# The combination of attention groups queued behind the first branch on three queues, inverse blocks loaded first, and the last two expert blocks multiplied together tile by tile

## The chip, the core and the metric

The kernel runs on one core of one Trainium2 chip. The metric is the device time of one execution in microseconds. TensorE (PE), VectorE (DVE), ScalarE (ACT), GpSimd (POOL) and SyncE (SP) each work through an instruction stream of their own in order, and wait for each other through semaphores. DMA transfers are issued by the streams of SP and ACT here (and by POOL for gathers); the profile shows an issuing stream as SPq or ACTq.

## What is computed

One layer of an encoder for 512 tokens of width 1024, in float32:

```python
xn = rmsnorm(h)
(dq, dk, dv, dz, da, db, aq, ak, av, gate_dn, gate_da) = split_columns(xn @ w_in, IN_WIDTHS)
o_dn = deltanet_branch(...)            # branch A: gated delta rule, two directions
o_da = dilated_attention_branch(...)   # branch B: three (window, dilation) groups of four heads
merged = sigmoid(gate_dn) * (o_dn @ w_branch_dn) + sigmoid(gate_da) * (o_da @ w_branch_da)
h = h + merged @ w_out
h = h + peer_ffn(rmsnorm(h), ...)      # 8 heads, top 16 of 16384 single-neuron experts
return rmsnorm(h, norm_final)
```

The attention branch ends with a combination: for each of its four heads the outputs of the three groups are weighted by a softmax over the groups and added.

```python
wts = jax.nn.softmax(jnp.stack(lses), axis=0)
o = jnp.einsum('gbhs,gbhsd->bhsd', wts, jnp.stack(outs))
```

## The kernel before

A float32 product is made of three matmuls (`mm3`): every operand is split into a high part, which ACT casts (`whi`, `xhi`, ..., line 117), and a low part, which DVE subtracts (`wlo`, ..., line 118); the products high-high, low-high and high-low are summed in PSUM. Weights come in halves of 128x1024 through SP (`raw`, line 147), three in flight.

The order of each engine's instructions is made by a tile scheduler from the code and a simulated timeline, not by the code's order alone. `keep_in_program_order` holds one instruction at its place, `issue_after` keeps what is issued in its scope behind a given instruction.

Around the change the stages on TensorE are, in order: the last projections with the attention of the last group; **branch A** (`branch_a`), whose input is transposed and split and then multiplied by `w_branch_dn`; the **gate blocks `gb`** (`gates(1, "gb")`), four blocks of two outputs of 128x512, each evicted by ACT as `f` (tanh, line 645); **branch da** (`branch` with `merge`), with the combination's result `obhi`, `oblo` as its input; and **w_out**.

- `branch` makes eight outputs of 12 matmuls of 128x512 (`mmb`, two PSUM banks). For branch A `keep` loads the gate into `pa` by ACT's queue (`pa<-th_d`, line 662, four buffers), multiplies on DVE (line 663), and stores by SP's queue (`pa_d<-pa`, line 664).
- The combination (lines 807 to 822) takes for each head h and group g the weights `cb<-c_d` (line 812, four buffers) and the group's output `og<-og_d` (line 814, six buffers) by SP's queue; DVE multiplies (line 815) and adds (line 819); the sum is split to `obhi` (ACT) and `oblo` (DVE). The first multiplication is held in program order.
- For branch da `fetch` loads `tb<-th_d` and `pa<-pa_d` by ACT's queue two outputs ahead (line 840); `merge` takes the product, adds `pa` and splits (`mhi`, `mlo`).
- w_out multiplies `mhi`, `mlo` in groups by token tile n into `mmo` (two banks, shared with `mmb`); `hs`, the input x as one load of 2 MB on ACT's queue (line 873), is added to the products.

Far ahead of this the delta rule inverts block triangular matrices. Per step, `m_d`, `i_d` and four diagonal blocks `e_d` are loaded by SP (lines 556 to 562).

At the program's end the expert outputs are summed over 64 blocks in six PSUM banks `acc[n][e]` (three token tiles, two halves), 36 matmuls of 128x512 a block (line 1201). In the last block these are sorted by tile, and behind each tile's 12 `final` adds `hs` (line 1162), takes the mean square (ACT), nine small operations for the inverse root (DVE, lines 181, 183, 108, 111 and 112), a scale by it and the norm's weights (line 1167) and the store.

## Time and profile before

| | |
|---|---|
| median of three runs | 1882.56 us (1878.89 to 1886.22) |
| the profiled execution | 1880.62 us, its span 1878.8 us |
| mean granted TensorE clock | 0.991 of full speed |
| TensorE busy | 1831.0 us (97%) |
| VectorE, ScalarE, GpSimd busy | 75%, 40%, 19% |

The span goes from the first to the last instruction of the profiled execution; the time holds 1.8 us more around it. Durations and starts below come from that one execution.

### The profile page before, as it was taken

Reading aid. Unit: us, or ns where it says so; the run is one execution under the profiler, and the core shown is the slowest. Engines: PE = TensorE matmul, PEld = TensorE weight load, DVE = VectorE, ACT = ScalarE, POOL = GpSimd, SP = SyncE. Lnnn points to the kernel's source line nnn. Section 1 sums busy time; section 2 is a strip of 40 time slices with the busy share of each in tenths; the row PEclk is TensorE's granted clock in tenths of the full one; section 3 lists DMA queues with packets and bytes.
Section 4 is the critical chain, followed back from the end, with each engine's and each line's share of the span. In section 5 each row is a group of like instructions: output and inputs, shape, how many; then the busy total and the mean of one; then the engine's idle time right before and its main releaser. Section 6 shows DMA issues by size and latency. Waiting matters only on the chain.

```text
span 1878.8 us, 28071 instructions
## 1 busy us (share of the span) xinstructions
PE 1831.0 (97%) x10438; PEld 1621.2 (86%) x10438; DVE 1400.7 (75%) x2979; ACT 751.5 (40%) x1168; POOL 364.1 (19%) x274
## 2 busy tenths in 40 slices
PE   8999999999699999999999999999999999999997
PEld 7897788888588888999999999999999998888886
DVE  6776544555535698999999857778778888787787
ACT  4543333343223423456666643333333332333332
POOL 0000000000000000001013223344444454233331
PEclk9999999999899999999999999999999999999999
DMA  6346423324865322557679899899999999999983
GB/s 204 101 133 180 135 85 94 102 86 144 281 210 163 130 90 85 166 160 283 238 282 377 317 384 327 293 350 332 338 345 321 352 321 368 378 351 345 337 306 125
DMA packets 188978, 451.84 MB, mean 240 GB/s; under 512 B 25053, under 2 KB 79901, under 8 KB 187306
## 3 DMA queue, kind: packets, MB, share of 16 engines
q1 hardware_dynamic: 135848, 266.75, 43.0%
q0 software_dynamic: 36864, 134.23, 19.5%
q10 hardware_dynamic: 16130, 49.07, 7.1%
q8 instruction: 82, 1.34, 0.3%
q14 instruction: 54, 0.44, 0.1%
HBM read 390.04 MB, written 59.96 MB: 240 GB/s over the span
## 4 chain that ended last, share of the span: by engine, by line
PE 62%; DMA 2%; DVE 1%; ACT 0%; issue 0%; SPq 0%; DVEq 0%; ACTq 0%
PE acc L1201 28%; PE psu L159 27%; PE psq L159 4%; PE psw L1123 2%; DMA wt<-w_d 1%; PE pssc L1007 1%; DMA raw<-peer_u 1%; DVE hs L1167 0%; DVE wlo L118 0%; ACT stage L1126 0%; SPq L147 0%; DVE hs L1162 0%; PE pst L1098 0%; DVE ge L1189 0%; ACT whi L117 0%
## 5 line engine op out<-in xcount | busy, mean ns | idle before, releaser
L118 DVE TENSOR_TENSOR wlo<-raw,whi 128x1024 fp32r<-128x1024 f32 x356 | 424.5, 1220 | 130.5 <-ACT whi L117 100.8
L117 ACT CAST whi<-raw 128x1024 fp32r<-128x1024 f32 x356 | 357.9, 1049 | 226.0 <-PE psu L159 76.4
L909 POOL DMA_INDIRECT grow<-peer_u_rows,gidx x128 | 175.5, 1371 | 834.8 <-DVE code L1046 497.7
L1201 PE MATMUL acc<-whi,hhi 128*128 128x512 f32 x768 | 237.1, 391 | 3.3 <-ACT hhi L117 3.3
L1201 PE MATMUL acc<-wlo,hhi 128*128 128x512 f32 x768 | 238.1, 390 | 0.0
L1201 PE MATMUL acc<-whi,hlo 128*128 128x512 f32 x768 | 237.2, 389 | 0.0
L909 POOL DMA_INDIRECT grow<-peer_v_rows,gidx x128 | 179.1, 1399 | 271.6 <-DVE gacc L928 242.9
L159 PE MATMUL psu<-x2hi,whi 128*128 128x384 f32 x1024 | 207.1, 341 | 0.0
L159 PE MATMUL psu<-x2lo,whi 128*128 128x384 f32 x1024 | 206.2, 340 | 0.0
L159 PE MATMUL psu<-x2hi,wlo 128*128 128x384 f32 x1024 | 205.5, 340 | 0.0
L117 ACT CAST hhi<-ge 128x768 fp32r<-128x768 f32 x64 | 53.6, 838 | 345.5 <-PE acc L1201 261.9
L159 PEld LDWEIGHTS psu<-x2hi,whi 128*128 128x128 f32 x1024 | 181.5, 188 | 2.8 <-ACT ge L964 0.6
L159 PEld LDWEIGHTS psu<-x2hi,wlo 128*128 128x128 f32 x1024 | 181.7, 188 | 0.0
L159 PEld LDWEIGHTS psu<-x2lo,whi 128*128 128x128 f32 x1024 | 181.4, 188 | 0.0
L1201 PEld LDWEIGHTS acc<-whi,hhi 128*128 128x128 f32 x768 | 144.3, 188 | 31.9 <-ACT hhi L117 3.6
L1201 PEld LDWEIGHTS acc<-wlo,hhi 128*128 128x128 f32 x768 | 144.7, 188 | 30.8
L1201 PEld LDWEIGHTS acc<-whi,hlo 128*128 128x128 f32 x768 | 144.2, 188 | 30.0
L928 DVE SCALAR_TENSOR_TENSOR gacc<-grow,gact,gacc 128x1024 f32<-128x1024 f32 x127 | 162.7, 1281 | 8.2 <-DMA grow<-peer_v_rows,gidx 6.7
L920 DVE SCALAR_TENSOR_TENSOR grow<-grow,x2g 128x1024 f32<-128x1024 f32 x128 | 152.2, 1220 | 13.5 <-DMA grow<-peer_u_rows,gidx 13.5
L159 PE MATMUL mmc<-xhi,whi 128*128 128x512 f32 (+1 forms) x528 | 135.6, 397 | 1.7 <-ACT xhi L117 1.2
L159 PE MATMUL mmc<-xhi,wlo 128*128 128x512 f32 (+1 forms) x528 | 133.6, 389 | 0.0
L159 PE MATMUL mmc<-xlo,whi 128*128 128x512 f32 (+1 forms) x528 | 131.9, 388 | 0.0
(355 smaller groups left out, 2427.5 us busy)
## 6 DMA issues: line engine op xcount, KB each, us to landing
raw<-peer_u SPq DMA_DIRECT2D x128, 512.0 KB
raw<-peer_v SPq DMA_DIRECT2D x128, 512.0 KB
raw<-w_in SPq DMA_DIRECT2D x68, 512.0 KB
w_d<-stage ACTq DMA_DIRECT2D x12, 2048.0 KB
wt<-w_d SPq DMA_DIRECT2D x32, 768.0 KB
ge_d<-ge SPq DMA_DIRECT2D x33, 384.0 KB
ge<-ge_d SPq DMA_DIRECT2D x33, 384.0 KB
raw<-peer_wq SPq DMA_DIRECT2D x16, 512.0 KB
```

Source lines behind the costliest of these rows:

```text
L117: S.copy(hi, src)
L118: sub = V.tensor_tensor(lo, src, hi.bitcast(F32), op=ALU.subtract)
L159: PE.matmul(ps, lhs(k)[x], rhs(k)[y], start=i == 0, stop=i == 3 * n - 1)
L909: G.indirect_dma_start(out=t_, out_offset=None, in_=rows, in_offset=bass.IndirectOffsetOnAxis(ap=gidx[:, slot:slot + 1], axis=0))
L920: tc.keep_in_program_order(V.scalar_tensor_tensor(t_, t_, 1.0, x2g, op0=ALU.mult, op1=ALU.mult, accum_out=gact[:, s:s + 1]))
L928: tc.keep_in_program_order(V.scalar_tensor_tensor(gacc, t_, gact[:, s:s + 1], gacc, op0=ALU.mult, op1=ALU.add))
L1007: PE.matmul(ps[:, n, :], qh[:, j, n * P:(n + 1) * P], sk[:, j, :], start=True, stop=True)
L1123: PE.matmul(ps[:, t, :], e1[:, pair, :, one], ge_[i][:, pair, :, one], start=i == 0, stop=i == 1)
L1201: PE.matmul(acc[n][e], x[:, j, n * P:(n + 1) * P], y[:, j, e * 512:(e + 1) * 512], start=b == order[0] and j == 0 and x is hhi and y is vh ...
```

## The change

1. *Inverse blocks:* the loads of the four diagonal blocks `e_d` are written ahead of those of `m_d` and `i_d`.
2. *Combination:* all of it is issued inside the scope of `issue_after` for three instructions of branch A: its last `pa<-th_d` load on ACT's queue, its last multiplication on DVE, its last `pa_d` store on SP's queue. The held multiplication is released.
3. *`hs`:* its load moves from the start of w_out into `fetch(KD - 1)`, behind the last `pa<-pa_d` load of the merge.
4. *Last two blocks:* the next to last block's 36 matmuls are kept back and sorted by tile together with the last block's 36; a tile ends after 24.

```diff
--- before.py
+++ after.py
@@ -553,13 +553,13 @@
                 xt = d2.tile([P, H, P], F32, name="xt", tag="xt")
                 yt = d2.tile([P, H, P], F32, name="yt", tag="yt")
                 mt = d2.tile([P, H, P], F32, name="mt", tag="mt")
-                nc.sync.dma_start(f4(mt), m_d[d, n])
-                it = d2.tile([P, H, P], F32, name="it", tag="it", bufs=1)
-                nc.sync.dma_start(f4(it), i_d[d, n])
                 dst, oth = (xt, yt) if d == 0 else (yt, xt)
                 G.memset(dst, 0.0)
                 for b in range(4):
                     nc.sync.dma_start(dst[diag[b], :, diag[b]], e_d[d, b, n].rearrange("h r c -> r h c"))
+                nc.sync.dma_start(f4(mt), m_d[d, n])
+                it = d2.tile([P, H, P], F32, name="it", tag="it", bufs=1)
+                nc.sync.dma_start(f4(it), i_d[d, n])
                 V.transpose(f4(oth), f4(dst))
                 zt = zts[:, d]
                 for wd in (32, 64):
@@ -654,14 +654,16 @@
                         lambda k: (hi[:, k, :], lo[:, k, :]), 4)
                     use(b * 4 + i, ps)
 
+        ends = [None] * 3
+
         def branch_a():
             d2ctx.close()
             with tc.tile_pool(name="oaT", bufs=1, side="right") as oap:
                 def keep(i, ps):
                     t_ = oap.tile([P, T], F32, name="pa", tag="pa", bufs=4)
-                    nc.scalar.dma_start(t_, th_d[0, i])
-                    V.scalar_tensor_tensor(t_, t_, 1.0, ps, op0=ALU.add, op1=ALU.mult)
-                    nc.sync.dma_start(pa_d[i], t_)
+                    ends[0] = nc.scalar.dma_start(t_, th_d[0, i])
+                    ends[1] = V.scalar_tensor_tensor(t_, t_, 1.0, ps, op0=ALU.add, op1=ALU.mult)
+                    ends[2] = nc.sync.dma_start(pa_d[i], t_)
 
                 oahi = oap.tile([P, H, T], F32R, name="oahi")
                 oalo = oap.tile([P, H, T], F32R, name="oalo")
@@ -805,6 +807,9 @@
         obhi = obp.tile([P, H, T], F32R, name="obhi")
         oblo = obp.tile([P, H, T], F32R, name="oblo")
         cmb = obctx.enter_context(tc.tile_pool(name="cmb", bufs=6, side="right"))
+        behind_a = ExitStack()
+        for last_a in ends:
+            behind_a.enter_context(tc.issue_after(last_a.ins))
         for h in range(H):
             for g in range(3):
                 c = g * 4 + h
@@ -812,14 +817,13 @@
                 nc.sync.dma_start(cb, c_d[c:c + 1].to_broadcast([P, T]))
                 og = cmb.tile([P, T], F32, name="og", tag="og")
                 nc.sync.dma_start(og, og_d[g * 4 + h])
-                mul = V.tensor_tensor(og, og, cb, op=ALU.mult)
-                if c == 0:
-                    tc.keep_in_program_order(mul)
+                V.tensor_tensor(og, og, cb, op=ALU.mult)
                 if g:
                     V.tensor_tensor(o_, o_, og, op=ALU.add)
                 else:
                     o_ = og
             split(obhi[:, h, :], oblo[:, h, :], o_)
+        behind_a.close()
 
         gates(1, "gb")
 
@@ -837,9 +841,12 @@
                 pair = []
                 for nm, src in (("tb", th_d[1, i]), ("pa", pa_d[i])):
                     t_ = m2.tile([P, T], F32, name=nm, tag=nm)
-                    nc.scalar.dma_start(t_, src)
+                    fetched = nc.scalar.dma_start(t_, src)
                     pair.append(t_)
                 ahead.append(pair)
+                if i == KD - 1:
+                    with tc.issue_after(fetched.ins):
+                        nc.scalar.dma_start(hs, a["x"].rearrange("(n p) d -> p n d", p=P))
 
             def merge(i, ps):
                 if i == 0:
@@ -869,8 +876,6 @@
             w = wblock(a["w_out"][e], (KD, 256))
             if e == 3:
                 wq0 = wblock(a["peer_wq"][0], (KD, 256))
-            if e == 0:
-                nc.scalar.dma_start(hs, a["x"].rearrange("(n p) d -> p n d", p=P))
             for n in range(NT):
                 tk = slice(n * P, (n + 1) * P)
                 ps = psa.tile([P, 256], F32, name="mmo", tag="mm", bufs=2)
@@ -1170,6 +1175,7 @@
             order = list(range(NF, NB)) + list(range(NF))
             new = dict(kept)
             new.update({b: layer1(b) for b in range(NF, NF + AHEAD)})
+            todo = []
             for b in order:
                 if NF <= b < NB - AHEAD:
                     new[b + AHEAD] = layer1(b + AHEAD)
@@ -1193,16 +1199,20 @@
                         pass
                     nc.sync.dma_start(gfin, a["norm_final"].to_broadcast([P, D]))
                     final(NT - 1, [gacc[:, e * 512:(e + 1) * 512] for e in range(2)])
-                todo = [(j, n, x, y, e) for j in range(2) for n in range(NT - 1)
-                        for x, y in ((hhi, vhi), (hhi, vlo), (hlo, vhi)) for e in range(2)]
+                todo += [(j, n, x, y, e) for j in range(2) for n in range(NT - 1)
+                         for x, y in ((hhi, vhi), (hhi, vlo), (hlo, vhi)) for e in range(2)]
+                if b == order[-2]:
+                    pace(2)
+                    continue
                 if b == order[-1]:
                     todo.sort(key=lambda q: (q[1], q[4]))
                 for i, (j, n, x, y, e) in enumerate(todo):
                     PE.matmul(acc[n][e], x[:, j, n * P:(n + 1) * P], y[:, j, e * 512:(e + 1) * 512],
                               start=b == order[0] and j == 0 and x is hhi and y is vhi,
-                              stop=b == order[-1] and j == 1 and x is hlo)
-                    if b == order[-1] and i % 12 == 11:
+                              stop=b == order[-1] and i % 12 == 11)
+                    if b == order[-1] and i % 24 == 23:
                         final(n, acc[n])
+                todo = []
                 pace(5 if b >= NF else 2)
     ctx.close()
```

What the change does to each engine's order: TensorE's is the same but for the last 72 matmuls, GpSimd's is the same. SP's differs in one place, the combination; its rows for the inverse blocks are the same. ACT's and DVE's differ around the combination, the merge and the end. At the end DVE's order is now: the last addition of `acc`, one small operation and the scale of the second tile, the nine small operations and the scale of the last tile; before, the scale of the first tile stood ahead of that addition, and the small operations of the second tile and its scale were mixed with those of the last.

SP, from the store of the combination's weights `ct` on, before:

```order
L804 DMA c_d<-ct 12x512
L814 DMA og<-og_d 128x512 x4
L812 DMA cb<-c_d 128x512 x4
L814 DMA og<-og_d 128x512
L664 DMA pa_d<-pa 128x512 x2
L814 DMA og<-og_d 128x512
L812 DMA cb<-c_d 128x512 x2
L664 DMA pa_d<-pa 128x512
L812 DMA cb<-c_d 128x512
```

and after the change:

```order
L806 DMA c_d<-ct 12x512
L666 DMA pa_d<-pa 128x512 x4
L147 DMA raw<-w_in 128x1024 x2
L666 DMA pa_d<-pa 128x512 x4
L817 DMA cb<-c_d 128x512
L819 DMA og<-og_d 128x512
L817 DMA cb<-c_d 128x512
L819 DMA og<-og_d 128x512
L817 DMA cb<-c_d 128x512
```

The stores `pa_d` of branch A were between the loads of the combination; now all eight are ahead of the first `cb`, with one weight block's two halves `raw` among them.

ACT from the load of `hs` on, before:

```order
L873 DMA hs<-x 128x4x1024
L117 CAST whi<-raw 128x1024 x2
L117 CAST obhi<-og 128x512
L662 DMA pa<-th_d 128x512 x3
L117 CAST obhi<-og 128x512
L662 DMA pa<-th_d 128x512
L117 CAST obhi<-og 128x512
L117 CAST whi<-raw 128x1024 x2
L117 CAST obhi<-og 128x512
L840 DMA pa<-pa_d 128x512 x3
L645 ACTIVATE f<-mmc 128x512
L117 CAST whi<-raw 128x1024 x2
```

and in the changed program, from the merge's first `pa` loads on, through the first gate outputs `f`:

```order
L844 DMA pa<-pa_d 128x512 x3
L645 ACTIVATE f<-mmc 128x512
L117 CAST whi<-raw 128x1024
L645 ACTIVATE f<-mmc 128x512
L117 CAST obhi<-og 128x512
L844 DMA tb<-th_d 128x512
L117 CAST obhi<-og 128x512
L645 ACTIVATE f<-mmc 128x512
L117 CAST whi<-raw 128x1024 x2
L844 DMA tb<-th_d 128x512
L645 ACTIVATE f<-mmc 128x512
L117 CAST whi<-raw 128x1024
```

Before, `hs` and four casts `obhi` (one for each head) stood around branch A's loads `pa<-th_d`, ahead of the first gate output `f`. Now the first two casts stand behind the second `f`, ahead of the third, and the other two further on.

ACT in the changed program at the last loads of the merge:

```order
L844 DMA pa<-pa_d 128x512
L849 DMA hs<-x 128x4x1024
L844 DMA tb<-th_d 128x512
L123 ACTIVATE mhi<-tb 128x512 x2
L117 CAST whi<-raw 128x1024 x2
```

`hs` stands between the last load `pa` and the last load `tb`.

DVE at the end of the merge and the start of w_out, before:

```order
L851 SCALAR_TENSOR_TENSOR tb<-tb,mmb 128x512 x2
L852 TENSOR_TENSOR tb<-tb,pa 128x512 x2
L124 SCALAR_TENSOR_TENSOR mlo<-tb,mhi 128x512 x2
L851 SCALAR_TENSOR_TENSOR tb<-tb,mmb 128x512
L118 TENSOR_TENSOR wlo<-raw,whi 128x1024
L852 TENSOR_TENSOR tb<-tb,pa 128x512
L118 TENSOR_TENSOR wlo<-raw,whi 128x1024
L124 SCALAR_TENSOR_TENSOR mlo<-tb,mhi 128x512
L879 TENSOR_TENSOR hs<-hs,mmo 128x256 x4
```

and after the change:

```order
L858 SCALAR_TENSOR_TENSOR tb<-tb,mmb 128x512 x2
L859 TENSOR_TENSOR tb<-tb,pa 128x512 x2
L124 SCALAR_TENSOR_TENSOR mlo<-tb,mhi 128x512 x2
L118 TENSOR_TENSOR wlo<-raw,whi 128x1024 x2
L858 SCALAR_TENSOR_TENSOR tb<-tb,mmb 128x512
L859 TENSOR_TENSOR tb<-tb,pa 128x512
L124 SCALAR_TENSOR_TENSOR mlo<-tb,mhi 128x512
L884 TENSOR_TENSOR hs<-hs,mmo 128x256 x4
```

The two halves `wlo` (of w_out's second block) stood between the operations of the last `tb`; now both are ahead of its first.

## Rows read from the trace of the kernel before

**Rows 1.** The page: the span, and part 1, engines' busy time.

```profile
span 1878.8 us, 28071 instructions
...
PE 1831.0 (97%) x10438; PEld 1621.2 (86%) x10438; DVE 1400.7 (75%) x2979; ACT 751.5 (40%) x1168; POOL 364.1 (19%) x274
```

**Rows 2.** Waits of TensorE: us in total, times, longest us.

```profile
PE mmb L159 <- DVE pa L663: 15.0, 2, 12.4
...
PE pz L576 <- DMA z<-z_d: 2.8, 1, 2.8
```

**Rows 3.** Timeline of TensorE: start us, us, operation, idle time before and what ended it.

```profile
491.08 1.10 PE L159 MATMUL mmb<-oahi,wlo 128*128 128x512 f32 x4
...
499.10 1.09 PE L159 MATMUL mmb<-oahi,whi 128*128 128x512 f32 x4
...
500.96 1.10 PE L159 MATMUL mmb<-oahi,wlo 128*128 128x512 f32 x4
...
514.45 2.08 PE L159 MATMUL mmb<-oahi,whi 128*128 128x512 f32 x4 [12.39 <-DVE pa L663]
...
521.94 2.01 PE L159 MATMUL mmc<-xhi,whi 128*128 128x512 f32 x8
...
532.86 0.39 PE L159 MATMUL mmc<-xhi,whi 128*128 128x512 f32 x1
```

**Rows 4.** Windows: us, each engine's busy time, granted clock, DMA share, GB/s.

```profile
495.00:500.00 5.00, 5.00 (x16) 3.96 (x17) 4.68 (x7) 0.62 (x1) 0.00 (x0) 0.71 1.03 416
...
585.00:590.00 5.00, 3.78 (x20) 2.96 (x19) 4.15 (x7) 2.26 (x4) 0.00 (x0) 1.00 0.36 133
```

**Rows 5.** Timeline of ScalarE and its queue, in two windows.

```profile
488.96 0.43 ACTq L873 DMA_DIRECT2D hs<-x  x1
...
506.48 2.97 ACTq L662 DMA_DIRECT2D pa<-th_d  x3
...
509.48 0.62 ACT L117 CAST obhi<-og 128x512 fp32r<-128x512 f32 x1 [11.01 <-DMA og<-og_d]
...
523.16 0.62 ACT L117 CAST obhi<-og 128x512 fp32r<-128x512 f32 x1
...
582.92 0.33 ACTq L840 DMA_DIRECT2D pa<-pa_d  x1
...
588.88 1.98 ACT L117 CAST whi<-raw 128x1024 fp32r<-128x1024 f32 x2
```

**Rows 6.** Waits of SyncE's queue: us in total, times, longest us.

```profile
SPq L814 <- DMA hs<-x: 5.3, 1, 5.3
```

**Rows 7.** Timeline of SyncE's queue.

```profile
485.53 1.75 SPq L812 DMA_DIRECT2D cb<-c_d  x4
...
503.45 0.32 SPq L814 DMA_DIRECT2D og<-og_d  x1
```

**Rows 8.** Timeline of VectorE, in two windows.

```profile
513.71 0.69 DVE L663 SCALAR_TENSOR_TENSOR pa<-pa,mmb 128x512 f32<-128x512 f32 x1 [1.55 <-DMA pa<-th_d]
...
589.62 0.68 DVE L851 SCALAR_TENSOR_TENSOR tb<-tb,mmb 128x512 f32<-128x512 f32 x1
...
591.95 1.22 DVE L118 TENSOR_TENSOR wlo<-raw,whi 128x1024 fp32r<-128x1024 f32 x1
```

**Rows 9.** Timeline of TensorE at the start of w_out.

```profile
591.85 0.28 PE L159 MATMUL mmo<-whi,mhi 128*128 128x256 f32 x1
```

**Rows 10.** Timeline of VectorE at the program's end.

```profile
1853.44 0.15 DVE L181 SCALAR_TENSOR_TENSOR tot<-ms 128x1 f32<-128x1 f32 x1
...
1855.36 1.42 DVE L1167 SCALAR_TENSOR_TENSOR hs<-hs,rs,x2g 128x512 f32<-128x512 f32 x2
...
1869.50 0.68 DVE L1162 TENSOR_TENSOR hs<-hs,acc 128x512 f32<-128x512 f32 x1
...
1874.22 1.42 DVE L1167 SCALAR_TENSOR_TENSOR hs<-hs,rs,x2g 128x512 f32<-128x512 f32 x2
```

**Rows 11.** Timeline of TensorE: the last matmul.

```profile
1867.99 0.39 PE L1201 MATMUL acc<-whi,hlo 128*128 128x512 f32 x1
```

## The prediction

> **What bounds the kernel now.** I read the page first: TensorE is busy 1831.0 of 1878.8 us [rows 1]. So an edit pays only where TensorE stands still, where its clock is low, or behind its last matmul; what other engines save elsewhere is hidden. The second view is TensorE's waits. One row stands out [rows 2]: two waits for the multiplication of branch A (`pa`, DVE), 15.0 us together, the longer 12.4. The third is TensorE's timeline there [rows 3]. A group of four branch matmuls takes 0.93 (500.96 less 499.10, two groups). [...]
>
> Why it stands is in the queues. ACT issues the 2 MB load `hs<-x` at 488.96 [rows 5], before branch A's last four loads of `th_d`. SP then waits 5.3 us for that load, ahead of an `og` load [rows 6], and goes on at 503.45 [rows 7]: 14.5 us from issue to landing. ACT issues the `th_d` loads at 506.48 [rows 5] and DVE, which has `og*cb` products among its `pa` operations, does the next `pa` at 513.71 [rows 8], where TensorE resumes (514.45). Thus the combination and `hs` stand in the way of branch A on all three queues.
>
> **The change part by part.**
>
> *Inverse blocks.* The order of issue on SP is the same in both programs, so the price is 0. The most an edit there could win is the one wait for `z_d`, 2.8 [rows 2]; losing needs a moved row, and there is none.
>
> *Combination and hs out of branch A.* Afterwards all eight `pa_d` stores precede the first `cb`, and the four loads follow the first four operations. What could still stop branch A: a store and then a load, both of the first buffer, between the first `pa` operation and the fifth. With two banks the fifth is due when the seventh output begins, five outputs of 12 matmuls (2.8 each) after the first output's end: 14.0, less two operations of 0.7, leaves 12.6 for the pair. The worst load took 7.2 (506.48 to 513.71), with combination loads beside it; so 5.4 are left for the store even then, and I take the pair as fitting. Lower end: one more stop like the shorter of the two, 15.0 less 12.4, 2.6. I take the full **-18.8**.
>
> *The combination, now late.* It no longer lies under branch A but under the `gb` gates, which don't need it until branch da. A `gb` block takes 10.92 (521.94 to 532.86 [rows 3]). With the loss gone `gb` starts at 503.2, and its blocks at 503.2, 514.1, 525.0 and 535.9; branch da is due at 546.8. The first `cb` is issued behind the last `pa` operation (0.7) and its store (0.3 of issue): about 504.4. ACT's new order is the risk: the casts `obhi` are interleaved with the casts of the next gate weights and with the `f` evictions that free TensorE's banks. Head 1's cast stands ahead of the second weight half of the third block, head 2's and 3's further on, so the third block (525.0) cannot go on without head 1. Before, from the first `cb` issue (485.53) to the cast of head 1 (509.48) passed 24.0, to that of head 3 (523.16) 37.6 [rows 5, 7]. [...] Head 3 at 542.0 is in time for 546.8. Below: 0, if DVE, free of its waits, is faster still. I take **+3.5**, between 0.3 and 7.5 and near their middle: the pace holds one removed wait, but DVE also does the gates' `wlo` subtractions there, and a stop of some length costs the clock besides. SP's `raw` loads now stand ahead of `cb`; they are due in any case.
>
> *hs as a neighbour of the merge.* `hs` is now issued between the last `pa` load and the last `tb` load of the merge. In the old times that is 583.3, just behind `pa` at 582.92 [rows 5]. Two things follow. First, DVE's order puts both `wlo` halves of the second output weight ahead of the last merge operation on `tb` (its last rows in the section on the change). That operation frees the bank into which the second tile's output group goes at 591.85 [rows 9], and ran at 589.62 [rows 8]. After, the two weight casts (588.88, 1.98 for both [rows 5]) end at 590.86, the second `wlo` (1.22 [rows 8]) at 592.2, and `tb` (0.7) at 592.9: a stop of **1.1** at least. Second, the last `tb` load lies behind 2.1 MB. At the 416 GB/s of 495 to 500 [rows 4] these take 5.0, from 583.3 to 588.3; if the weight loads take half of the rate, until 593.3. Then come `tb`'s own 0.26 MB (0.6) and the operation (0.7): 589.6 or 594.6, so the stop is 1.1 or 2.8. [...] I take **+2.5**, near the shared rate: the 14.5 were spent where the DMA engines' share was 1.03 (495 to 500), and from 585 to 590 it is 0.36 without `hs` [rows 4].
>
> [...]
>
> What `hs` and the combination leave behind: w_out's sum needs `hs` after its first group, later than `tb`, so no further wait.
>
> *Last two blocks together.* 72 matmuls instead of 36 are sorted by tile, so a tile ends every 24 matmuls, not 12; their count and duration stay. The last block's data is needed earlier: its first matmul comes 22 into the 72, so 50 x 0.23 (a quarter of 0.93) ahead of the end, at 1856.9; its last `hlo` subtraction is done when DVE goes on at 1853.44 [rows 10] or just behind, 3 us ahead, so that costs nothing. Before, TensorE ends at T = 1867.99 + 0.39 = 1868.4 [rows 11]; DVE adds the last tile at 1869.50, 1.1 late, busy until then with the scale of the first tile, and ends its last scale at 1874.22 + 1.42 = T + 7.3, with the second tile's scale in between [rows 10]. After, the add starts at T + 0.05 (0.6), then 0.2 of the second tile's chain, its scale (1.34), nine small operations of the last tile (1.92, 1853.44 to 1855.36 [rows 10]) and the last scale (1.42): T + 5.5. **-1.7.** Bounds: -2.4 if that second scale, too, is out of the way by T (its matmuls end 24 x 0.23 = 5.4 before); -0.4 if six small operations of the second tile (1.3) still come behind T.
>
> *Sum.* The profiled execution took 1880.6 us. 1880.6 - 18.8 + 3.5 + 2.5 - 1.7 = 1866.1. The median of the three runs is 1.9 above that execution: **1868**.
>
> **The rivals.**
>
> [...]
>
> [...]
>
> [...]
>
> C. *Slower.* With no branch work between them, the twelve `cb` loads go through four buffers in three rounds, and SP stands in each round for a transfer, as it did once, 5.3 [rows 6]. Such waits shift the heads and, through ACT's order, the gates behind them. If they take the place of the +3.5, three of 6.0 ((18.8 + 1.7 - 2.5) / 3) use up the gain; from 9.1 each it is slower by over 0.5%, and three of 10 give 1895. For it: SP has waited 5.3 for one transfer. Against it: that was for 2 MB, and these are 256 KB each.
>
> D. *Nothing gained in branch A*, because the store and load of the buffers are slow by themselves (the 7.2 of rows 5 and 8 is not due to `hs`): three stops of 2.6 remain of the 18.8 and it ends at 1876.
>
> **How the numbers follow.** About 0.5%, 9.4 us, is what a measurement of this kernel can tell from no change: the border is 1873. Chances: the forecast 0.66, A 0.13, B 0.10, both or D 0.08, C 0.03. The likeliest has 1868. Its best corner: 1880.6 - 18.8 + 0 + 1.1 - 2.4 = 1860.5, in the median's terms 1862.4; the runs before scatter by 3.7 either way, so 1859 is the lower end. Upwards the range takes in A and the middle of B, 1876, and leaves out C, A and B together, and half of B and D, 0.15 in all. Faster: the forecast and nearly all of A, 0.78; same: B, both, D and the rest of A, 0.19; slower: C, 0.03.
>
> **What would show it.** Right: TensorE's waits hold no `mmb` for `pa` of over 1 us, and the groups of branch A run at 0.93; `gb` begins about 503. A wait of TensorE at the third `gb` block for an `f` eviction or `whi`, 0 to 5.6, sizes the term of the combination; one of an `mmo` for `tb`, 1 to 4, that of `hs`; the span's end less the last matmul, 10.8 before (1878.8 - 1868.0), is to be 9.1. Wrong: waits of `pa` that remain (D), a `tb` that waits for its load over 5 us (B), SP rows on `cb` of over 5 us each (C), or a new wait in a stage that the change does not touch.

## The result

| | median, us | runs | ratio to before, 95% interval |
|---|---|---|---|
| before | 1882.11 | 4 (1878.89 to 1886.22) | |
| after | 1870.28 | 4 (1864.55 to 1871.48) | 0.9930 (0.9902 to 0.9958) |
| after, a second time on another occasion | 1869.79 | 6 (1865.40 to 1874.60), before then 1882.13 | 0.9929 (0.9912 to 0.9947) |

The changed kernel is 12 us, 0.7%, faster. 1868 was forecast, with 1859 to 1876 as the range.

The profiled execution of the changed kernel took 1864.55 us and is the quickest of its four; its profile is read with that in mind. The page, with its span and the busy times of part 1:

```profile
span 1862.8 us, 28073 instructions
...
PE 1827.6 (98%) x10438; PEld 1618.9 (87%) x10438; DVE 1401.4 (75%) x2979; ACT 751.0 (40%) x1168; POOL 358.0 (19%) x274
```

16.0 less than in [rows 1], of which TensorE was busy 3.4 less: the rest it no longer stands idle. Its waits (us in total, times, longest us) answer to [rows 2]:

```profile
PE mmc L159 <- ACT f L645: 3.4, 1, 3.4
...
PE mmb L159 <- DVE tb L858: 2.1, 1, 2.1
...
PE pz L576 <- DMA z<-z_d: 2.1, 1, 2.1
...
PE mmo L159 <- DVE tb L858: 1.8, 1, 1.8
```

The two waits of branch A for `pa` (15.0) are gone. In their place two new rows stand: 3.4 for `f` in the gate blocks, and 1.8 of w_out for `tb`. The wait for `z_d` (2.1) is 0.7 shorter than before, with SP's order there unchanged; such differences are told of below. TensorE's timeline through branch A and the gates (start, us, instruction, idle time ahead of it and what ended it):

```profile
490.45 1.10 PE L159 MATMUL mmb<-oahi,wlo 128*128 128x512 f32 x4
...
491.38 1.09 PE L159 MATMUL mmb<-oahi,whi 128*128 128x512 f32 x4
...
499.79 2.01 PE L159 MATMUL mmc<-xhi,whi 128*128 128x512 f32 x8
...
525.14 3.48 PE L159 MATMUL mmc<-xhi,whi 128*128 128x512 f32 x8 [3.39 <-ACT f L645]
...
528.46 2.00 PE L159 MATMUL mmc<-xlo,whi 128*128 128x512 f32 x8
```

The branch's groups now follow each other at 0.93 without a break (490.45 to 491.38), where [rows 3] had a stop of 12.4 and behind it four matmuls in 2.08, at a granted clock of 0.50 (514.5 to 518.3). The `gb` blocks begin at 499.79. The stop is in the third block, at 525.14: 3.39 of standing, and then eight matmuls in 3.48 where the next eight take 2.00, at a granted clock of 0.50 (525.2 to 528.0) and 1.00 (528.7 to 530.0), so the clock cost 1.5 more.

I divide each profiled execution at the same five places of TensorE's timeline: the first `mmb` of branch A, the first `mmc` behind its last `mmb`, the first `mmb` of branch da, the first `mmo`, and the end of the last `acc`. The lengths between them, in us, for all the kernels of this study (the last column is good to about 0.05, since spans are given to 0.1):

| kernel | starts at | branch A | gate blocks | branch da | w_out to last matmul | last matmul to span's end |
|---|---|---|---|---|---|---|
| before | 479.35 | 42.59 | 43.56 | 23.90 | 1278.98 | 10.42 |
| **after** | 475.91 | 23.88 | 48.63 | 24.82 | 1280.88 | 8.68 |
| after, again | 481.94 | 23.86 | 51.96 | 26.05 | 1280.38 | 8.61 |
| combination alone | 479.84 | 30.91 | 51.06 | 25.77 | 1277.07 | 10.45 |
| hs alone | 477.93 | 30.95 | 45.37 | 24.63 | 1283.00 | 10.42 |
| last two blocks alone | 479.32 | 43.16 | 45.42 | 25.90 | 1280.46 | 8.64 |
| inverse loads alone | 480.57 | 43.51 | 43.85 | 26.04 | 1279.75 | 10.48 |
| merge loads late | 479.99 | 23.87 | 43.56 | 26.54 | 1280.05 | 8.79 |
| hs a stage earlier | 479.89 | 23.87 | 50.51 | 26.18 | 1276.69 | 8.76 |
| both of these | 481.30 | 23.88 | 43.56 | 29.89 | 1279.63 | 8.74 |
| tb from another source | 477.14 | 23.87 | 46.15 | 25.81 | 1281.52 | 8.61 |
| merge loads late, hs in quarters | 479.39 | 23.88 | 43.56 | 28.52 | 1280.43 | 8.52 |
| only tb late, hs in quarters | 478.84 | 23.88 | 45.40 | 24.39 | 1278.86 | 8.53 |
| the same, quarters later | 478.50 | 23.88 | 44.54 | 26.14 | 1279.02 | 8.52 |

From before to after: 3.44 in the start, 18.71 in branch A, -5.07 in the gates, -0.92 in branch da, -1.90 behind it and 1.74 at the end make the 16.0. Up to branch A no kernel of the table changes the order of any engine, and the start still lies between 475.9 and 481.9; from w_out's first matmul on, the length lies between 1277.1 and 1281.5 in the kernels whose TensorE order there is that of before or of after (hs alone, 1283.0, and hs a stage earlier, 1276.7, have orders of their own). So 3.4 of the 16.0 in the profiled executions belong to no edit, and what is left, 12.6, agrees with the medians' 11.8. The -1.90 has w_out's new wait for `tb`, 1.8, in it, but lies within the scatter as well.

### The profile page after: what moved, and what is told of

It reads as the page before. It is cut to its first block, busy times and chain, and to the rows that moved or that the text cites. A ratio compares the mean times of both kernels' runs of the same rounds, so it can differ in the third digit from the quotient of the medians.

```text
span 1862.8 us, 28073 instructions
## 1 busy us (share of the span) xinstructions
PE 1827.6 (98%) x10438; PEld 1618.9 (87%) x10438; DVE 1401.4 (75%) x2979; ACT 751.0 (40%) x1168; POOL 358.0 (19%) x274
## 4 chain that ended last, share of the span: by engine, by line
PE 57%; issue 5%; DMA 2%; POOL 1%; DVE 1%; SPq 0%; ACT 0%; DVEq 0%; POOLq 0%; ACTq 0%
PE acc L1210 28%; PE psu L159 22%; PE psq L159 4%; PE psw L1128 1%; POOL grow L914 1%; DMA wt<-w_d 1%; PE pssc L1012 1%; DMA grow<-peer_u_rows,gidx 1%; DVE wlo L118 0%; DVE grow L925 0%; DVE hs L1172 0%; DVE eg L1121 0%; DVE e L1117 0%; DVE e L1116 0%; SPq L147 0%
## 5 line engine op out<-in xcount | busy, mean ns | idle before, releaser
L914 POOL DMA_INDIRECT grow<-peer_v_rows,gidx x128 | 174.8, 1366 | 275.4 <-DVE gacc L933 248.0
```

The lines of the kernel that those rows point to most:

```text
L914: G.indirect_dma_start(out=t_, out_offset=None, in_=rows, in_offset=bass.IndirectOffsetOnAxis(ap=gidx[:, slot:slot + 1], axis=0))
```

## The experiments

**Each part alone.** Four kernels apply one part of the change to the kernel before. The combination alone:

```diff
...
+        behind_a = ExitStack()
+        for last_a in ends:
+            behind_a.enter_context(tc.issue_after(last_a.ins))
...
-                mul = V.tensor_tensor(og, og, cb, op=ALU.mult)
-                if c == 0:
-                    tc.keep_in_program_order(mul)
+                V.tensor_tensor(og, og, cb, op=ALU.mult)
...
+        behind_a.close()
```

> Only the combination is queued behind branch A; hs keeps its place on ACT's queue ahead of branch A's last four loads. Theory 1 (the stops in branch A come from the combination's loads and products among branch A's, and hs's 2 MB make them worse): no wait of the first kind (2.6 before) is left, the second is 0 to 7 (hs lands 6 to 14.5 us after its issue, the fifth pa operation is due 8 after it), the gate stop with its clock is the 5.1 of the changed kernel, the merge is as before: 18.8 less 0 to 9, less 5.1, so 5 to 14 faster than before. Rival (hs alone makes the stops): the wait of 12 stays, and with the gate stop it is 2 to 5 slower than before.

Measured: 1875.75 against 1883.11, ratio 0.9961 (0.9945 to 0.9977). TensorE's waits, and ACT's queue at branch A:

```profile
PE mmc L159 <- ACT f L645: 5.3, 1, 5.3
...
PE mmb L159 <- DVE pa L665: 4.3, 1, 4.3
```

```profile
486.15 0.39 ACTq L877 DMA_DIRECT2D hs<-x  x1
...
494.64 4.08 ACTq L664 DMA_DIRECT2D pa<-th_d  x4
```

The first kind of stop is gone, and 4.3 is left of the 12.4. `hs` is still issued ahead of branch A's last four loads `pa<-th_d`, which begin at 494.64 here and at 484.83 in the changed kernel. Theory 1 held; the gates' stop (5.3, and 7.5 in the stage) was above what I expected.

hs alone:

```diff
...
+                if i == KD - 1:
+                    with tc.issue_after(fetched.ins):
+                        nc.scalar.dma_start(hs, a["x"].rearrange("(n p) d -> p n d", p=P))
...
-            if e == 0:
-                nc.scalar.dma_start(hs, a["x"].rearrange("(n p) d -> p n d", p=P))
```

> Only hs moves behind the last pa load of the merge; the combination stays among branch A's rows. Theory 1: the first stop (2.6, for combination loads) stays and the second shrinks from 12.4 to under 6, so 6 to 14 of the 18.8 come back, less 2.9 for the merge and w_out: 3 to 11 faster than before. Rival (the combination alone makes the stops): both stops stay at 15 and it is 3 slower than before. Rival 2 (hs alone makes them): both stops go, 16 faster.

Measured: 1872.36 against 1883.11, ratio 0.9954 (0.9934 to 0.9974). TensorE's waits, and VectorE's timeline at the first stop:

```profile
PE mmb L159 <- DVE pa L663: 4.0, 2, 3.5
...
PE mmo L159 <- DVE tb L854: 1.9, 1, 1.9
```

```profile
489.96 0.69 DVE L815 TENSOR_TENSOR og<-og,cb 128x512 f32<-128x512 f32 x1 [4.08 <-DMA cb<-c_d]
...
492.89 0.69 DVE L815 TENSOR_TENSOR og<-og,cb 128x512 f32<-128x512 f32 x1 [2.24 <-DMA og<-og_d]
...
493.50 0.68 DVE L663 SCALAR_TENSOR_TENSOR pa<-pa,mmb 128x512 f32<-128x512 f32 x1
```

Now the other half is left: `pa` at 493.50 stands on DVE behind two products that waited for `cb` and `og`. A third wait for `pa`, of 1.5, falls into the gates, whose 45.37 contain it. Theory 1 held, both rivals fell. Either part alone leaves about 7.1 of branch A's 18.7 (30.91 and 30.95 against 23.88): each gives 11.7, and both 18.7, not the sum. The two causes made each other worse: `hs` held SP's combination loads (5.3, [rows 6]), and beside the combination's traffic `hs` itself took longer. By the traces' landing events, which tell when the last part of a transfer is there, `hs` landed 14.4 us after its issue before, and 10.0 with the combination behind branch A.

The last two blocks alone (the diff's last two hunks), and the inverse loads alone (its first):

> Only the last two expert blocks are multiplied together. From the last matmul's end to the span's end 8.7 instead of 10.4: 1.7 faster than before, all else within its scatter. Rival: the last block's data are late and TensorE waits for hhi or hlo between the blocks, 0 or slower.

> Only the e_d loads are written ahead of m_d and i_d. SP's order of issue is that of before, so the time is the same within the scatter of the runs (0.2%), and the first stages move by a few us either way from one execution to the next. Rival: the 3.4 us by which the changed kernel's profiled execution was ahead of before's at the start of branch A come from this part, and it is 3 faster.

Measured: 1881.17, ratio 0.9994 (0.9984 to 1.0004), and 1884.11, ratio 1.0003 (0.9989 to 1.0018), both against 1883.11. The end of the first is 8.64 where 10.42 was: 1.8 less, as expected, though the runs alone can't tell 0.1% from nothing. The second shows nothing, and its branch A starts at 480.57, later than before's: the start's 3.4 is not the inverse blocks'.

**The stop in the gates.** In the changed kernel ACT's queue reads (first casts of the heads, and the `f` for which TensorE waits):

```profile
514.69 0.62 ACT L117 CAST obhi<-og 128x512 fp32r<-128x512 f32 x1 [3.19 <-DVE og L822]
...
523.60 0.33 ACTq L844 DMA_DIRECT2D tb<-th_d  x1
...
523.97 0.62 ACT L117 CAST obhi<-og 128x512 fp32r<-128x512 f32 x1 [8.66 <-DMA og<-og_d]
...
524.50 0.59 ACT L645 ACTIVATE f<-mmc 128x512 f32<-128x512 f32 x1
```

Head 1's sum was done on DVE by 519.6:

```profile
518.17 1.41 DVE L822 TENSOR_TENSOR og<-og 128x512 f32<-128x512 f32 x2
```

but its cast came at 523.97, since a load `tb` of the merge stood ahead of it until 523.60. In the compiled program that load waits on two completion counters (the order of the program has eight, 0 to 7, which the transfers of SP and ACT take in turn): counter 5, its data's store `th_d<-f`, and counter 1, last taken by a load `og` of SP's queue. The rows of the order with their waits, ACT's and then SP's:

```
390 L117 CAST obhi<-og 128x512 [waits DVE_49]
391 L844 DMA tb<-th_d 128x512 [waits DMAHW5_49,DMAHW1_49]
392 L117 CAST obhi<-og 128x512 [waits DVE_49]
393 L645 ACTIVATE f<-mmc 128x512 [waits PE_49,Activation_49]

213 L819 DMA og<-og_d 128x512 [waits DMAHW1_49,DVE_49]
```

SP issued that `og` at 515.99:

```profile
515.99 0.46 SPq L819 DMA_DIRECT2D og<-og_d  x1
```

at a time when the DMA engines' busy share was 1.01 to 1.03 (windows: us, busy times, granted clock, DMA share, GB/s):

```profile
514.00:520.00 6.00, 6.00 (x29) 4.95 (x27) 5.55 (x8) 0.62 (x1) 0.00 (x0) 1.00 1.01 347
...
520.00:525.00 5.00, 1.75 (x8) 1.13 (x6) 0.38 (x1) 1.03 (x3) 0.00 (x0) 0.97 1.03 375
```

and the load landed some 7.6 us later. The trace's landing events put the store on counter 5 at 518.82 and the `og` on counter 1 at 523.58, 0.02 ahead of the issue of `tb`: it was the other queue's load that held ACT, which had a cast and an eviction ready behind it. The store alone would have let `tb` go before head 1's sum was done.

Three kernels on the changed one test this, beside the changed kernel itself. The first holds the merge's loads behind the last head's cast, the second moves `hs` there, the third does both. All three write the split out as in the first hunk, to have a name for the cast:

```diff
-            split(obhi[:, h, :], oblo[:, h, :], o_)
+            cast = S.copy(obhi[:, h, :], o_)
+            V.tensor_tensor(oblo[:, h, :], o_, obhi[:, h, :].bitcast(F32), op=ALU.subtract)
...
-                    fetched = nc.scalar.dma_start(t_, src)
+                    with tc.issue_after(cast.ins):
+                        fetched = nc.scalar.dma_start(t_, src)
```

```diff
-                if i == KD - 1:
-                    with tc.issue_after(fetched.ins):
+                if i == 0:
+                    with tc.issue_after(cast.ins):
                         nc.scalar.dma_start(hs, a["x"].rearrange("(n p) d -> p n d", p=P))
```

> The changed kernel itself once more, as the measure for the three beside it: 12 us faster than before, branch A 23.9 us, the gate blocks 48 to 49 with one stop of 3 to 5 for an f eviction, the w_out group's wait for tb 1.8, 8.7 from the last matmul's end to the span's end.

> The changed kernel with the merge's tb and pa loads of ACT's queue behind the cast of the last head. Theory 1 (the gate stop comes from a tb load on ACT's queue that cannot be issued until an og load of SP has landed, ahead of head 1's cast and of an f eviction; the sum of head 1 was ready at 519.6, 2.2 before TensorE stood): the stop for f falls from 3.4 to under 1, the gate blocks take 43.6 to 44.6 instead of 48.6, 4 to 5 faster than the changed kernel. Rival (the combination itself is too slow, at the DMA engines' limit): the stop stays at 3 or more, behind obhi, and the gate blocks at 47 or more.

> The changed kernel with hs's load behind the cast of the last head, a stage earlier than the merge's last loads; DVE's order at w_out is then that of before. Theory 1 (the wait of w_out's second group for tb, 1.8, comes from hs in front of the last tb load, 0.9, and from the two wlo ahead of that tb, 1.0): it goes to 0, and the time is 1.8 to 2.3 less than the changed kernel's. Rival (hs costs wherever it stands, since the loads share 16 engines): a wait of 1 to 3 shows in branch da or the gates in its place, and the time is the same.

> Both edits on the changed kernel: the merge's first loads and hs behind the last head's cast. If theory 1 holds for both, 6 to 7 less than the changed kernel, 18 to 19 less than before, about 1863 to 1864; TensorE's stages: branch A 23.9, gate blocks 44, branch da 24 to 26, no wait of w_out for tb. Rival (loads moved to one place get in each other's way): a new wait for tb or for pa in branch da of 2 or more, and 3 less than the changed kernel at most.

Measured, against 1882.13: the changed kernel 1869.79, 0.9929 (0.9912 to 0.9947); merge loads late 1863.39, 0.9898 (0.9881 to 0.9915); hs earlier 1867.80, 0.9923 (0.9906 to 0.9940); both 1866.22, 0.9910 (0.9890 to 0.9931).

The changed kernel's second profile has the stop longer than expected, 5.7; the rows of TensorE, VectorE and ACT there:

```profile
533.49 3.78 PE L159 MATMUL mmc<-xhi,whi 128*128 128x512 f32 x8 [5.74 <-ACT f L645]
...
526.44 1.41 DVE L822 TENSOR_TENSOR og<-og 128x512 f32<-128x512 f32 x2
...
521.39 0.62 ACT L117 CAST obhi<-og 128x512 fp32r<-128x512 f32 x1 [3.88 <-DVE og L822]
...
531.96 0.33 ACTq L844 DMA_DIRECT2D tb<-th_d  x1
...
532.32 0.62 ACT L117 CAST obhi<-og 128x512 fp32r<-128x512 f32 x1 [10.31 <-DMA og<-og_d]
...
532.85 0.59 ACT L645 ACTIVATE f<-mmc 128x512 f32<-128x512 f32 x1
```

ACT is free from 522.0 and issues `tb` at 531.96, and the cast and `f` follow at once; `og` on counter 1 landed at 531.93, the store on counter 5 at 527.09. But here head 1's sum, too, was late, at 527.85, 0.1 behind the beginning of TensorE's stop. With the cast (0.53 to the next start) and `f` (0.59) behind it, I estimate a stop of 1.3 without the queue's wait, so some 4.4 of the 5.7 are the queue's. With the merge's loads behind, head 1's cast and the same `f` come as they are ready:

```profile
521.73 0.62 ACT L825 CAST obhi<-og 128x512 fp32r<-128x512 f32 x1 [3.17 <-DVE og L822]
...
523.53 0.59 ACT L645 ACTIVATE f<-mmc 128x512 f32<-128x512 f32 x1
```

and the gate blocks take 43.56, to the hundredth what they took before. Theory 1 held: in this profile, and in two more below with 43.56, the combination fits under the gates, and the stop was the queue's. The kernel is 6.4 faster than the changed one by the medians, and the runs hardly overlap (1859.80 to 1865.59 against 1865.40 to 1874.60).

hs a stage earlier: the wait of w_out for `tb` is gone. DVE's order is again that of before, one `wlo` behind the last `tb` and not two ahead:

```profile
580.65 0.69 DVE L859 SCALAR_TENSOR_TENSOR tb<-tb,mmb 128x512 f32<-128x512 f32 x1 [1.73 <-PE mmb L159]
...
581.25 1.22 DVE L118 TENSOR_TENSOR wlo<-raw,whi 128x1024 fp32r<-128x1024 f32 x1
```

but of the 2.0 by which the median is lower the intervals cannot be sure. The gates' stop is still there, and the queue's: `tb` was issued at 528.13, 0.02 after the `og` on counter 1 had landed, with head 1's sum ready since 523.97. With both edits it came out as the rival said: TensorE's waits have a row of three stops in branch da,

```profile
PE mmb L159 <- DVE tb L860: 5.1, 3, 3.4
```

and the stage takes 29.89, 3.4 more than with the merge loads alone. The loads of the merge and the 2 MB are now issued together, from 539.05 on; that this is what makes the stops is likely, but no run separates it.

**Is it the counter or the data?** The next kernel lets the first three `tb` loads read branch A's gates, which were stored long before, so that they depend on no store of this stage (its output is then not the layer's). On ACT's queue they stand behind the first head's cast, ahead of an eviction and of head 1's cast:

```diff
...
+            cast0 = cast if h == 0 else cast0
...
+                    with tc.issue_after(cast0.ins) if nm == "tb" else ExitStack():
-                        fetched = nc.scalar.dma_start(t_, src)
+                        fetched = nc.scalar.dma_start(t_, th_d[0, i] if nm == "tb" and i < 3 else src)
```

> The changed kernel with the merge's first three tb loads reading branch A's gates (stored long ago) in place of their own, so that they need no store of this stage; on ACT's queue they stand behind the first head's cast, ahead of an f eviction and head 1's cast; the output is not the reference's. What is left that they can wait for is the landing of the transfer that last used their completion counter. Theory 1 (that landing is what held the tb load): ACT still stands in front of a tb load for 3 or more, the f eviction behind it comes late, and the gate blocks take 46 to 53. Rival (the store of th_d was the late one): no stop for f over 0.5, gate blocks 43.6 to 44.5.

Measured: 1864.40 against 1882.19, ratio 0.9905 (0.9888 to 0.9922). ACT's rows, at these loads and at the gates' one longer stop, and that stop on TensorE:

```profile
515.54 0.62 ACT L825 CAST obhi<-og 128x512 fp32r<-128x512 f32 x1 [2.81 <-DVE og L822]
...
518.70 3.55 ACTq L847 DMA_DIRECT2D tb<-th_d  x3
...
522.38 0.60 ACT L645 ACTIVATE f<-mmc 128x512 f32<-128x512 f32 x1 [6.22 <-DMA raw<-w_in]
...
534.98 0.62 ACT L825 CAST obhi<-og 128x512 fp32r<-128x512 f32 x1 [3.82 <-DVE og L822]
...
535.51 0.59 ACT L645 ACTIVATE f<-mmc 128x512 f32<-128x512 f32 x1
```

```profile
536.15 2.11 PE L159 MATMUL mmc<-xhi,whi 128*128 128x512 f32 x8 [1.38 <-ACT f L645]
```

ACT is free at 516.16 and has issued the three loads by 522.25, 6 us for 1 us of issuing, and the 6.22 of idle time ahead of `f` are put down to a weight load of SP's queue; the data of these `tb` had long been stored. In this kernel's order the three wait on the counters 2, 4 and 6, last taken by a `cb`, an `og` and a `raw` of SP's queue; by the landing events these landed at 518.68, 520.00 and 521.90, and the `tb` were issued at 518.70, 520.02 and 521.93. So another queue's transfer on the same counter does hold ACT, and theory 1's half on ACT is shown. Its half on the gates is not: `f` at 522.38 came nearly in time, and TensorE's next matmul began at 523.03, some 0.2 late. Of the 2.6 that the gates' 46.15 are above 43.56, the larger part is the stop at 536.15, for an `f` behind head 2's cast, which waited for DVE's sum and not for a `tb`. That the length lies within what theory 1 expected is luck.

**A better place for hs.** Two kernels, with the merge's loads held back as above, split `hs` into four loads of 0.5 MB, one behind each of four merge pairs; the second holds back only the `tb` loads, and a third is the second with the quarters one pair later.

```diff
-                if i == KD - 1:
+                if 2 <= i < 6:
                     with tc.issue_after(fetched.ins):
-                        nc.scalar.dma_start(hs, a["x"].rearrange("(n p) d -> p n d", p=P))
+                        nc.scalar.dma_start(hs[:, i - 2, :], a["x"][(i - 2) * P:(i - 1) * P, :])
```

> The merge's first loads behind the last head's cast, and hs as four loads of 0.5 MB, one behind each of the third to sixth pair of merge loads. If branch da's new stops with hs in one piece came from 2 MB in front of the small loads, branch da takes 25 to 27 (29.9 with one piece), w_out's wait for tb is 0, and the time is 0 to 2 below that of the merge loads' edit alone: 19 to 21 less than before. Rival (it is the sum of bytes, not the piece): branch da 28 or more, no faster than that edit alone.

> As the one beside it, but only the tb loads are held behind the last head's cast, the first three pa loads stay early, and with them the first quarter of hs, ahead of the combination's casts. Three loads fewer stand at the start of branch da: 24 to 26 there. The early quarter adds 1.3 us of transfer (0.5 MB at about 400 GB/s) to the combination's stretch: gate blocks 43.6 to 45. Rival (the DMA engines are full there and head 1 has no slack): a stop of 1 to 3 for f or whi in the gate blocks, and slower than the one beside it.

> The last kernel with hs's four quarters behind the fourth to seventh pair of merge loads, so that none is issued in the combination's stretch. If the early quarter made the gate blocks 45.4 rather than 43.6, they are 43.6 to 44.2 now; branch da 24 to 26 as before the edit, no wait of w_out for tb: 1 to 2 below the last kernel, 21 to 23 less than before. Rival (the three early pa loads did it): the gate blocks stay at 45 or more and the time is the same.

Measured: 1862.54, 0.9892 (0.9876 to 0.9908), and 1861.85, 0.9895 (0.9880 to 0.9911), both against 1882.19; the third 1865.20 against 1883.18, 0.9910 (0.9892 to 0.9928). In the first, branch da takes 28.52, as the rival said: the sum of bytes fits better than the single piece. In the second it takes 24.39, and the gates lose 1.8, more than the forecast allowed (its 1.3 is an estimate, at a rate between the 347 to 375 GB/s above and the 416 of [rows 4]), in two stops of TensorE smaller than the rival's 1 to 3:

```profile
525.95 1.19 PE L159 MATMUL mmc<-xhi,whi 128*128 128x512 f32 x4 [0.35 <-ACT whi L117]
...
537.11 2.11 PE L159 MATMUL mmc<-xhi,whi 128*128 128x512 f32 x8 [0.89 <-ACT f L645]
```

The third gives half of that back, between its forecast and its rival, and loses it in branch da. None is told apart from the merge loads' edit alone (0.9898) by its interval. About 1862 to 1866, 16 to 20 below before and 4 to 8 below the changed kernel, is what all versions with the late merge loads reach.

## Right or wrong, by its steps

*Branch A, -18.8.* The term is, in [rows 3], the 30.86 from 491.08 to 521.94 less 13 groups of 0.93. Right in size: 18.71 in the profile (42.59 to 23.88), and the same length within 0.02 in all kernels that have both parts. Of the 18.71, 15.0 were the two stops [rows 2]; the other 3.7 lie in the slower matmuls behind them (2.08 for four behind the longer one, where 1.10 is usual [rows 3]). The story of three queues was right as well; that the two causes overlap, and each alone is worth 11.7, it did not say. It also left open why an `og` should wait for `hs`, which it does not read: in the order before, that `og` waits on counter 0, last taken by `hs`, and ACT's first late `pa<-th_d` on counter 7, last taken by a `cb` of SP's queue. By the landing events `hs` landed at 503.37 and the `cb` at 506.40, 0.08 ahead of the two issues at 503.45 [rows 7] and 506.48 [rows 5]; the store that freed the buffer of that `pa` had landed by 499.66. The wait that held the gates later was thus already part of branch A's long stop; how much of the 12.4 it made no run separates.

*The combination under the gates, +3.5.* This is the term that was mis-sized, and its mechanism was wrong where it measured head 1 by the pace of before, 24.0 from the first `cb` issue to the cast. No run shows the term or its bounds, 0.3 and 7.5, which were the author's estimates; 5.1, 8.4 and (hs earlier) 7.0 were lost against the 43.56 of before. 5.1 is nearer the term, the other two are nearer 7.5. But it was not the pace that made them: in the first profile head 1's sum was ready at 519.6, 2.2 ahead of TensorE's stop at 521.75, and in hs earlier it was as early (523.97, with the stop from 525.72); only in the second profile, where it was ready at 527.85, has the pace a share, about 1.3 of the 5.7. What was late stood in the order's rows between the two casts, the load `tb`, which I read past as an instruction without a price. The clock added the rest, as in the rows of before: 1.5 behind the stop of 3.39 (from 525.0 to 528.6 the granted clock was 0.56).

*hs as a neighbour of the merge, +2.5.* Near in the first profile, where w_out waits 1.8 for `tb`; in the second it waits 0.7, below the 1.1 that was to be the least. ACT, DVE and TensorE at that place:

```profile
564.03 1.53 ACTq L844 DMA_DIRECT2D tb<-th_d  x2
...
566.21 0.52 ACTq L849 DMA_DIRECT2D hs<-x  x1
...
567.22 0.33 ACTq L844 DMA_DIRECT2D tb<-th_d  x1
```

```profile
569.58 1.28 DVE L858 SCALAR_TENSOR_TENSOR tb<-tb,mmb 128x512 f32<-128x512 f32 x2 [2.39 <-DMA tb<-th_d]
...
573.71 2.36 DVE L118 TENSOR_TENSOR wlo<-raw,whi 128x1024 fp32r<-128x1024 f32 x2 [0.25 <-ACT whi L117]
...
576.95 0.69 DVE L858 SCALAR_TENSOR_TENSOR tb<-tb,mmb 128x512 f32<-128x512 f32 x1 [0.87 <-DMA tb<-th_d]
```

```profile
577.69 0.39 PE L159 MATMUL mmo<-whi,mhi 128*128 128x256 f32 x1 [1.84 <-DVE tb L858]
```

Both `wlo` (573.71 to 576.07) stand ahead of the last `tb`, and a wait of 0.87 for its load follows, as the two steps had it. The load was issued at 567.22, just behind `hs`, and landed 9.7 later; the two issued at 564.03, ahead of `hs`, were there at 569.58, within 5.6. The two issued ahead of `hs` landed before it and the one behind it after it (`hs` at 576.01, that `tb` at 576.92). Whether the order of issue made that `tb` late the trace does not show: at the 346 GB/s moved from 566 to 573 the 2.1 MB take 6 us in whatever order. The wait of branch da for `tb` (2.1, 1.2 before) I had left unchanged; it is 1.8 with the last two blocks alone and 3.1 with the combination alone, where `hs` is early, so its 0.9 more can't be put down to `hs`.

*Last two blocks, -1.7.* Right: 1.74, 1.81 and 1.78 in three pairs of profiles. TensorE's last matmul and VectorE behind it answer to [rows 10, 11]:

```profile
1853.73 0.39 PE L1210 MATMUL acc<-whi,hlo 128*128 128x512 f32 x1
```

```profile
1854.15 0.69 DVE L1167 TENSOR_TENSOR hs<-hs,acc 128x512 f32<-128x512 f32 x1 [0.54 <-PE acc L1210]
...
1854.95 1.42 DVE L1172 SCALAR_TENSOR_TENSOR hs<-hs,rs,x2g 128x512 f32<-128x512 f32 x2
...
1856.28 0.15 DVE L181 SCALAR_TENSOR_TENSOR tot<-ms 128x1 f32<-128x1 f32 x1
...
1858.19 1.42 DVE L1172 SCALAR_TENSOR_TENSOR hs<-hs,rs,x2g 128x512 f32<-128x512 f32 x2
```

The last addition starts 0.03 after the last matmul's end (1854.12), then come one small operation, the second tile's scale, the nine and the last scale, in the order and at the prices of the sum; a next gain there, not tried, would be that scale ahead of the nine.

*Inverse blocks, 0.* Right: 1.0003.

*The sum.* 1868 against 1870.28 and 1869.79; the gates' 1.6 to 4.9 above their term are the difference, and with 7.5 in place of 3.5 the sum, 1872, is as near. That the sum came so close is in part luck: the hs term came out lower than forecast, 1.8 and 0.7, where the gates' came out higher. B, C and D did not come about: TensorE waited for no `tb` over 2.1 in the changed kernel, no `cb` held SP for over 2.6, and no stop for `pa` was left.

## What to carry to other kernels

In this program an instruction that only issues a transfer has a price on its engine's queue: by the compiled order it waits for the data, and for whatever last used its completion counter, also on another queue, and everything behind it on that queue waited along (6 us for three loads whose data had long been stored, issued 0.02 to 0.03 behind the landings of another queue's transfers). These waits stand in the compiled order and can be read there ahead of any run. When a change makes one queue busier, look on every other compute queue for issues that stand ahead of a cast or an eviction; moving those behind gave as much here (6.4) as half of the whole change. Of two causes that stop the same place, each removed alone can give a large part of the gain that they share (here 11.7 and 11.7 of 18.7), so parts tested singly do not add up.

## What the runs showed of the hardware

ACT did no work for 8.7 and 10.3 us around the issue of one load of 256 KB, which went out 0.02 and 0.03 after a transfer of SP's queue on the same counter had landed; in the first of these profiles the DMA engines moved 347 to 375 GB/s meanwhile, at a share of 1.01 to 1.03. In both the cast of the next head followed the load by 0.37 and 0.36, and `f` followed the cast by 0.53.

What the matmuls behind a stop took was not of one size: behind 2.12 (branch da, after) four took 1.21, at a granted clock of 1.00 (570.3 to 571.5), behind 2.32 (merge loads late) 2.08, behind 1.96 (hs earlier) 1.75, where 1.10 is usual. What decided it the rows don't tell.

Executions of one order differ by up to 6 us before branch A, 475.9 to 481.9, and their waits for transfers with them (`z_d` 1.3 to 2.8); that is half of this change's worth, and a single profile's span says little about a change of this size.
